# The vector engine's part of a depthwise convolution: one running sum in PSUM in place of two in SBUF

## The chip, the cores and the metric

The kernel runs on one core of a Trainium2 chip. The metric is the device time of one execution in microseconds (us), and lower is better. The engines of the core are TensorE (PE in the profile), VectorE (DVE), ScalarE (ACT), GpSimd (POOL) and SyncE (SP), which issues transfers. SBUF is the on-chip memory that all of them use; PSUM is the small memory, here used as eight banks of 128 partitions by 512 fp32 values, into which TensorE writes its products.

## The reference

Two streams of 256 tokens each, the latent tokens and a context, with 1024 channels in fp32, pass two layers: half a gated FFN, a token mixer, half a gated FFN. The mixer of layer 0 is a convolution module, that of layer 1 an attention; a final norm ends the latent stream. The change lies in the convolution module:

```
def conformer_conv(h, pw1_w, pw1_b, dw_w, dw_b, ln_g, ln_b, pw2_w, pw2_b):
    a = h @ pw1_w + pw1_b
    u, g = jnp.split(a, 2, axis=-1)
    u = u * jax.nn.sigmoid(g)
    u = lax.conv_general_dilated(
        u, dw_w[:, None, :].astype(u.dtype), window_strides=(1,),
        padding=[(CONV_PAD, CONV_PAD)], dimension_numbers=("NWC", "WIO", "NWC"),
        feature_group_count=D_MODEL) + dw_b
    uf = u.astype(jnp.float32)
    mu = jnp.mean(uf, axis=-1, keepdims=True)
    var = jnp.mean(jnp.square(uf - mu), axis=-1, keepdims=True)
    u = ((uf - mu) * lax.rsqrt(var + NORM_EPS)).astype(u.dtype) * ln_g + ln_b
    return jax.nn.silu(u) @ pw2_w + pw2_b
```

Each of the 1024 channels is convolved over time with 31 weights of its own (`dw_w`). Context and latent tokens are convolved separately.

## The kernel before

**Layout.** Channels lie on the 128 partitions, in eight chunks (c = 0 to 7); the free axis holds 512 tokens, latent first. Every matrix product in fp32 is three products of high and low halves (`mm3`: hi·hi, hi·lo, lo·hi). Weights come in by DMA, ACT writes the high half (`hi`), GpSimd subtracts it from the raw value (`lo`).

**The convolution module.** `pw1_mm` makes the products of the first pointwise layer for one chunk: a tile `u` and a tile `g`, each one PSUM bank (`ug` in the trace). `pw1_end` is the GLU: ACT takes the sigmoid of `g` (`sg`), VectorE multiplies it with `u` into the padded tile `U` in SBUF. After that U's chunk is convolved. The eight chunks are divided among the engines:

- VectorE takes chunks 0, 2 and 3 whole and the latent half of chunk 4 (its first 256 columns); it runs one SCALAR_TENSOR_TENSOR for each tap: the shifted U times the tap's weight, plus a running sum (`taps_v`).
- ACT and GpSimd take chunk 1 (`taps_p`): ACT multiplies, GpSimd adds.
- TensorE takes chunks 5, 6 and 7 and the context half of chunk 4 (`taps_t`), after `split_u` has split U into high and low halves.

In `taps_v` the running sum of a chunk is kept twice, in `A_`, which is the chunk's place in the result tile `Dt`, and in `B`, a work tile; both lie in SBUF. Even taps go to A_, odd ones to B. ACT makes the first tap of each (L706, L708). For chunks 3 and 4 the tap 1 also subtracts the mean shift K0 (L719). Chunk 0's first 20 taps (KS) go over each stream's 256 columns by themselves; everything else is 512 wide, and chunk 4's half 256. At the end L727 adds A_ and B; for chunk 2 L732 subtracts K0. Then `stats` adds the chunk to a running sum (L686), ACT squares it (L688), and VectorE adds the squares some taps later (L689).

**K0.** When chunk 0 is ended, `shift` (K) sums it over its partitions on TensorE (L935, output `pn`), and ACT writes K0 from that (L936, shown as `SK<-pn`). `first_stats` (D) subtracts K0 from chunk 0. The other chunks get K0 subtracted in `centre` (L819, L822) or as told above. `ln_stat` (s, L829) is the matmul on the finished sums, with which the LayerNorm of the latent stream begins.

**What sets the order.** Inside the convolution no scheduler works: a string of tokens, `SEQ2`, is run from left to right, and each engine gets its instructions in that order. `A`, `C` and `P` are the pointwise products of the latent half of chunks 0 and 1, the context half of these, and both halves of a later chunk; `l`, `m` and `E` are their GLUs; `v1` is one tap of VectorE from the queue `qv`, which holds the chunks 0, 2, 3 and 4 in turn; `R1` is a pair of taps of chunk 1; `T` are taps on TensorE; `L` and `h` load a weight block; `S` splits U; `K`, `D`, `F`, `s` as above. So a stretch around the end of chunk 0 reads `v1 v1 v1 h v1 L K v1 R1 v1 ...`, and an instruction that waits holds up all that comes after it on its engine. Outside the convolution a scheduler orders the work by dependencies and by the tiles that pools have free.

**Banks.** The pool `ps` has six PSUM banks in turn for all products (`ug`, and `o` of TensorE's taps), `pn` two for norms and statistics.

Of the kernel before, what the change touches and what calls it, by code (L numbers as in the profile page):

```python
# [11 lines left out]
F32 = mybir.dt.float32  # L12
# [3 lines left out]
ALU = mybir.AluOpType  # L16
# [69 lines left out]
def trunk(ctx, tc, a, out):  # L86
# [8 lines left out]
    small = ctx.enter_context(tc.tile_pool(name="small", bufs=2))  # L95
    ps = ctx.enter_context(tc.tile_pool(name="ps", bufs=6, space=bass.MemoryType.PSUM))
    pn = ctx.enter_context(tc.tile_pool(name="pn", bufs=2, space=bass.MemoryType.PSUM))
# [27 lines left out]
    def pcol(off, i):  # L125
        return par[:, off + i:off + i + 1]

# [1 line left out]
    stream = []  # L129
# [90 lines left out]

# [1 line left out]
    todo = [(0, t) for t in range(16, 72)] + [(1, t) for t in range(72)]  # L222
# [19 lines left out]

# [1 line left out]
    accj = const.tile([P, 2 * T], F32, name="accj")  # L244
# [98 lines left out]

# [1 line left out]
    XG = []  # L345
# [115 lines left out]

# [1 line left out]
    R0 = work.tile([P, 2, T], F32, tag="mt", name="R0")  # L463
# [3 lines left out]
    b1 = const.tile([P, CT], F32, name="b1")  # L467
    gu = [[ps.tile([P, 512], F32, tag="ps", name="gu") for _ in range(2)] for _ in range(NFF0)]
    chunks = []
# [64 lines left out]
    with tc.manual_schedule(engines=MS):  # L534
# [31 lines left out]
        def root(s):  # L566
            r = rs[s]
            nc.vector.tensor_reduce(out=r, in_=pc[:, 4 * s:4 * s + 4].rearrange("p (b h) -> p b h", h=2),
                                    axis=mybir.AxisListType.X, op=ALU.add)
            nc.gpsimd.tensor_tensor(out=r, in0=r, in1=nhalf[:, 0:2], op=ALU.pow)  # L570
# [55 lines left out]

# [1 line left out]
    ffn(0, 0, (0, 1), pre_ctx=None, mid=lambda: norm(0, 0, 1), per_block=lambda: ada(2 + (done[0] % 5 == 0)), begun=gu)  # L628

# [1 line left out]
    Dt = mp.tile([P, CT, 2 * T], F32, tag="mh", name="Dt")  # L631
# [9 lines left out]
    def pw1_mm(cs, kts, sl, first=True):  # L641
        """Products of the blocks cs over kts, all outputs of a kt before the next."""
        for kt in kts:
            for blk, u, g in cs:
                hi, lo = blk
                for q, dst in enumerate((u, g)):
                    o = (q * 8 + kt) * P
                    mm3(dst[:, :sl.stop - sl.start], hi[:, o:o + P], lo[:, o:o + P], HH[:, kt, sl], HL[:, kt, sl], kt == 0, kt == 7)
# [22 lines left out]
    def wk(c, k):  # L671
        return pcol(O_DWW, c * CW + k)

    def dview(c, a_, b_):
        return Dt[:, c, a_ * T:b_ * T].rearrange("p (s t) -> p s t", t=T)
# [15 lines left out]
    def step(n=1):  # L691
        for z in lag:
            z[0] -= n
        while lag and lag[0][0] <= 0:
            lag.pop(0)[1]()

    def taps_v(c, a_, b_, ks=0):
        A_ = dview(c, a_, b_)
        Bt = work.tile([P, 512], F32, tag="mt", name="B")
        B_ = Bt[:, a_ * T:b_ * T].rearrange("p (s t) -> p s t", t=T)  # L700

        def src(k, z=slice(a_, b_)):
            return UV[:, c, z, k:k + T]

        def first(z, d, e):
            nc.scalar.activation(out=d, in_=src(0, z), func=AF.Identity, scale=wk(c, 0), bias=pcol(O_DWB, c))  # L706
            if c in (0, 2):
                nc.scalar.activation(out=e, in_=src(1, z), func=AF.Copy, scale=wk(c, 1))  # L708
        if ks:
            for s in range(2):  # L710
                first(slice(s, s + 1), A_[:, s:s + 1], B_[:, s:s + 1])
                for k in range(2, ks):
                    d = (A_ if k % 2 == 0 else B_)[:, s]
                    nc.vector.scalar_tensor_tensor(out=d, in0=src(k, s), scalar=wk(c, k), in1=d, op0=ALU.mult, op1=ALU.add)
                    yield
        else:
            first(slice(a_, b_), A_, B_)
        if c not in (0, 2):
            nc.vector.scalar_tensor_tensor(out=B_, in0=src(1), scalar=wk(c, 1),  # L719
                                           in1=K0[:, a_ * T:b_ * T].rearrange("p (s t) -> p s t", t=T),  # L720
                                           op0=ALU.mult, op1=ALU.subtract)
            yield
        for k in range(max(2, ks), CW):
            d = A_ if k % 2 == 0 else B_
            nc.vector.scalar_tensor_tensor(out=d, in0=src(k), scalar=wk(c, k), in1=d, op0=ALU.mult, op1=ALU.add)  # L725
            yield
        nc.vector.tensor_tensor(out=A_, in0=A_, in1=B_, op=ALU.add)  # L727
        if c == 0:
            return
        yield  # L730
        if c == 2:
            nc.vector.tensor_tensor(out=Dt[:, c, :], in0=Dt[:, c, :], in1=K0, op=ALU.subtract)  # L732
            yield
        stats(c, a_, b_)
# [90 lines left out]
    def ln_stat(s):  # L825
        pc = pn.tile([P, 512], F32, tag="pn", name="pn")
        for z, o in ((S1[:, SL[s]], 0), (acc[s], 2)):
            for b in range(2):
                nc.tensor.matmul(pc[:, o + b:o + b + 1], z[:, b * P:(b + 1) * P], k1024, start=True, stop=True)  # L829
        return pc  # L830
# [64 lines left out]
    with tc.manual_schedule(engines=MS):  # L895
# [3 lines left out]
        def put(k, *v):  # L899
            st[k] = v[0] if len(v) == 1 else v  # L900
# [31 lines left out]

        def shift():
            pk = pn.tile([P, 512], F32, tag="pn", name="pn")
            nc.tensor.matmul(pk, ones, Dt[:, 0, :], start=True, stop=True)  # L935
            nc.scalar.activation(out=K0, in_=pk, func=AF.Copy, scale=1.0 / P)  # L936
# [5 lines left out]
        def tap(c, n):  # L942
            gen = st.setdefault(("t", c), taps_t(c))
            for _ in range(n):
                next(gen, None)

        def root():
# [11 lines left out]
            "F": lambda v: centre(v // 100, v // 10 % 10, v % 10), "Q": lambda c: stats(c, 0, 2), "z": step,  # L959
            "s": lambda _: put("pc", ln_stat(0)), "q": lambda _: root(), "M": lambda _: bcast(st["m"], st["R"][:, T:]),  # L960
            "W": lambda _: bcast(st["r"], st["R"]), "n": lambda c: put(("n", c), ln_scale(0, c, st["R"])),
            "o": lambda c: ln_low(0, c, st.pop(("n", c)))}
        for t in SEQ2.split():
            ops[t[0]](int(t[1:] or 0))
        st = None
    UHL.clear()
# [10 lines left out]

# [1 line left out]
    ffn(0, 2, (0, 1), pre_ctx=lambda: norm(1, 0, 2), mid=lambda: norm(0, 1, 0), per_block=lambda: ada(1))  # L979
    ffn(1, 0, (0, 1), pre_ctx=lambda: norm(1, 1, 0), mid=lambda: norm(0, 1, 1), per_block=lambda: ada(2))  # L980

# [1 line left out]
    cst = rawp.tile([P, 2048], F32, tag="raw", name="cst")  # L983
# [136 lines left out]

# [1 line left out]
    sq = ffn(1, 2, (0,), pre_ctx=None, mid=None, per_block=lambda: ada(1))  # L1122
# [112 lines left out]
```

## Time and profile before

| what | value |
|---|---|
| time of the runs | 1762.5, 1767.8, 1770.88 us; median 1767.8 us |
| span of the profiled execution, first to last instruction | 1767.2 us; it has no other time of its own, and is 0.6 us below the median |
| TensorE matmuls busy over the span | 1677.1 us (95%) |
| VectorE busy | 1193.3 us (68%) |
| GpSimd busy | 824.0 us (47%) |
| ACT busy | 632.4 us (36%) |
| mean granted clock of TensorE | 0.970 of full speed |

The span is one profiled execution, whose parts can be read; the runs' times are what a change is measured by. Shares over the whole span are means over stages with different limits. A row of the timeline gives a start and a duration, and in brackets how long the engine had been idle before, and the instruction that ended the wait.

### The profile page before, as it was taken

To read this page: it belongs to the slowest core of one execution; us is meant where nothing else is said; L and a number is where in the kernel's file an instruction comes from. 1 tells how busy PE (TensorE), PEld (TensorE's weight loads), DVE (VectorE), ACT (ScalarE), POOL (GpSimd) and SP (SyncE) were. 2 spreads that over 40 slices of the span, in tenths; PEclk is the share of its full clock that TensorE was granted. 3 is DMA by queue.
4 is the path that set the end of the run, shared out by engine and by line. 5 is a ranking of instruction groups with operands and counts; after the bars stand their busy time and mean duration, and the time that the engine had idled before them with its cause. 6 is when DMAs were issued, how large, how long until landed. Compare 5 with 4: busy or idle time off the path is not lost.

```text
span 1767.2 us, 23475 instructions
## 1 busy us (share of the span) xinstructions
PE 1677.1 (95%) x9229; PEld 1436.1 (81%) x9229; DVE 1193.3 (68%) x1792; ACT 632.4 (36%) x1074; POOL 824.0 (47%) x577
## 2 busy tenths in 40 slices
PE   8999999999676798999999999999999999989998
PEld 7788888879566698888888898888888897789997
DVE  3588889877999887554555565755553389756562
ACT  2522222234423574322222233212222346745443
POOL 1234223364867565656566555565565454230003
PEclk7999999999888899999999999999999999989999
DMA  7645466442112232434333332454553221236451
GB/s 268 227 168 217 180 218 238 175 149 73 48 48 95 96 132 96 153 133 142 132 137 134 134 119 97 190 185 166 182 190 111 90 72 49 74 128 229 171 194 66
DMA packets 48494, 252.13 MB, mean 143 GB/s; under 512 B 5248, under 2 KB 7296, under 8 KB 30848
## 3 DMA queue, kind: packets, MB, share of 16 engines
q1 hardware_dynamic: 48384, 250.64, 39.6%
q8 instruction: 72, 1.18, 0.3%
q14 instruction: 38, 0.31, 0.1%
HBM read 249.57 MB, written 1.05 MB: 142 GB/s over the span
## 4 chain that ended last, share of the span: by engine, by line
PE 70%; DVE 18%; issue 5%; ACT 3%; DMA 2%; POOL 2%; SPq 0%; POOLq 0%; DVEq 0%; ACTq 0%
PE o L213 8%; PE o L214 8%; PE o L215 8%; PE g L214 7%; PE g L215 7%; PE u L214 7%; PE g L213 7%; PE u L215 7%; PE u L213 7%; DVE Dt L725 3%; DVE B L725 3%; DVE junk L235 2%; PE gu L530 2%; POOL lo L177 1%; ACT hi L174 1%
## 5 line engine op out<-in xcount | busy, mean ns | idle before, releaser
L177 POOL TENSOR_TENSOR lo<-raw,hi 128x512 fp32r<-128x512 f32 (+1 forms) x416 | 639.3, 1567 | 706.5 <-ACT hi L174 566.2
L174 ACT ACTIVATE hi<-raw 128x1024 fp32r<-128x1024 f32 (+3 forms) x364 | 296.8, 872 | 577.7 <-PE u L214 254.8
L235 DVE CUSTOM_DVE_ANT_0 junk<-adaw,srow,par 128x1024 bf16<-128x1024 f32 x224 | 382.0, 1705 | 6.6 <-DMA adaw<-in_adaT 2.0
L213 PE MATMUL o<-MH,hi 128*128 128x512 f32 (+1 forms) x788 | 269.7, 344 | 4.3 <-ACT MH L218 4.3
L214 PE MATMUL o<-ML,hi 128*128 128x512 f32 (+1 forms) x788 | 269.8, 344 | 0.0
L215 PE MATMUL o<-MH,lo 128*128 128x512 f32 (+1 forms) x788 | 269.7, 344 | 0.0
L214 PE MATMUL g<-HL,hi 128*128 128x512 f32 (+1 forms) x712 | 254.8, 358 | 4.0 <-DVE HL L324 4.0
L213 PE MATMUL g<-HH,hi 128*128 128x512 f32 (+1 forms) x712 | 253.8, 358 | 3.1 <-ACT HH L320 3.1
L215 PE MATMUL g<-HH,lo 128*128 128x512 f32 (+1 forms) x712 | 254.4, 357 | 0.0
L215 PE MATMUL u<-HH,lo 128*128 128x512 f32 (+1 forms) x712 | 254.3, 357 | 0.0
L214 PE MATMUL u<-HL,hi 128*128 128x512 f32 (+1 forms) x712 | 254.3, 357 | 0.0
L213 PE MATMUL u<-HH,hi 128*128 128x512 f32 (+1 forms) x712 | 253.8, 357 | 0.0
L219 DVE TENSOR_TENSOR ML<-mt,MH 128x512 fp32r<-128x512 f32 (+1 forms) x92 | 104.7, 1138 | 120.8 <-ACT MH L218 120.5
L393 DVE TENSOR_TENSOR mt<-sg,u 128x512 f32<-128x512 f32 (+1 forms) x89 | 53.0, 596 | 179.6 <-PE u L215 163.1
L213 PEld LDWEIGHTS o<-MH,hi 128*128 128x128 f32 x788 | 149.2, 190 | 22.7 <-ACT MH L218 5.2
L341 DVE SCALAR_TENSOR_TENSOR X<-o,g,X 128x256 f32<-128x256 f32 x168 | 75.4, 479 | 131.7 <-PE o L215 131.5
L215 PEld LDWEIGHTS o<-MH,lo 128*128 128x128 f32 x788 | 149.8, 190 | 17.6
L214 PEld LDWEIGHTS o<-ML,hi 128*128 128x128 f32 x788 | 149.7, 190 | 17.7
L214 PEld LDWEIGHTS g<-HL,hi 128*128 128x128 f32 x712 | 134.0, 189 | 26.9 <-DVE HL L324 5.3
L213 PEld LDWEIGHTS g<-HH,hi 128*128 128x128 f32 x712 | 134.2, 189 | 25.8 <-ACT HH L320 4.3
L213 PEld LDWEIGHTS u<-HH,hi 128*128 128x128 f32 x712 | 134.4, 189 | 21.6
L215 PEld LDWEIGHTS g<-HH,lo 128*128 128x128 f32 x712 | 134.4, 189 | 21.6
(208 smaller groups left out, 2676.1 us busy)
## 6 DMA issues: line engine op xcount, KB each, us to landing
raw<-in_wi SPq DMA_DIRECT2D x85, 1024.0 KB, 4.8
adaw<-in_adaT SPq DMA_DIRECT2D x128, 512.0 KB, 3.7
raw<-in_wo SPq DMA_DIRECT2D x32, 896.0 KB, 4.7
raw<-in_wo SPq DMA_DIRECT2D x20, 1024.0 KB, 5.2
raw<-in_pw SPq DMA_DIRECT2D x12, 1024.0 KB, 4.8
raw<-in_dwd SPq DMA_DIRECT2D x8, 1024.0 KB, 4.8
ch<-in_ada SPq DMA_DIRECT2D x6, 1024.0 KB, 12.7
raw<-in_qkv SPq DMA_DIRECT2D x6, 1024.0 KB, 4.8
```

The source lines that it names most:

```text
L174: nc.scalar.activation(out=hi[:, q:q + w], in_=raw[:, q:q + w], func=AF.Copy)
L177: eng.tensor_tensor(out=lo[:, z:e], in0=raw[:, z:e], in1=hf[:, z:e], op=ALU.subtract)
L213: nc.tensor.matmul(o, wh, xh, start=first, stop=False)
L214: nc.tensor.matmul(o, wh, xl, start=False, stop=False)
L215: return nc.tensor.matmul(o, wl, xh, start=False, stop=last)
L219: return i_, nc.vector.tensor_tensor(out=lo, in0=src, in1=hif, op=ALU.subtract)
L235: nc.vector.tensor_tensor_reduce(out=junk, in0=wt, in1=srow[:, s, :], scale=1.0, scalar=pcol(O_ADAB, 72 * l + t), op0=ALU.mult, op1=ALU.ad ...
L341: return nc.vector.scalar_tensor_tensor(out=X[:, c, SL[s]], in0=psrc, scalar=gate, in1=X[:, c, SL[s]], op0=ALU.mult, op1=ALU.add)
L393: nc.vector.tensor_tensor(out=mt[:, :n], in0=sg[:, :n], in1=u[:, :n], op=ALU.mult)
L530: nc.tensor.matmul(gu[k][q], w[:, o:o + P], h[:, c, :], start=c == 0 and h is HH and w is hi, stop=c == 7 and w is lo)
L725: nc.vector.scalar_tensor_tensor(out=d, in0=src(k), scalar=wk(c, k), in1=d, op0=ALU.mult, op1=ALU.add)
```

## The change

The pool `ps` gets five banks, and a new pool `pv` one: it holds a tile `A`, in which VectorE keeps a single running sum. Every tap of `taps_v` reads A and writes A in place; tap 0 is a TENSOR_SCALAR on VectorE (U times its weight), so ACT's first taps are gone, and so are B and the addition at the end. When the taps of a chunk have ended, one instruction writes Dt from A: for chunk 0 it adds the bias, for the others it adds the bias and subtracts K0 in one SCALAR_TENSOR_TENSOR. As the next chunk uses the same bank, its tap 0 waits for that instruction. The number of yields in a chunk's taps has changed, so a `v1` late in the string stands for another tap than before: `K` now runs VectorE's taps until chunk 0 has ended, and `s` first runs what is left. At the start of the kernel one tile of the first FFN's products (`gu`) lies in the new pool. The rest of the diff is comments that are left out.

```
-    ps = ctx.enter_context(tc.tile_pool(name="ps", bufs=6, space=bass.MemoryType.PSUM))
+    ps = ctx.enter_context(tc.tile_pool(name="ps", bufs=5, space=bass.MemoryType.PSUM))
+    pv = ctx.enter_context(tc.tile_pool(name="pv", bufs=1, space=bass.MemoryType.PSUM))
...
-    gu = [[ps.tile([P, 512], F32, tag="ps", name="gu") for _ in range(2)] for _ in range(NFF0)]
+    gu = [[pv.tile([P, 512], F32, tag="pv", name="gu") if 2 * k + q == 5 else ps.tile([P, 512], F32, tag="ps", name="gu")
+           for q in range(2)] for k in range(NFF0)]
...
+    ended = set()
+
     def taps_v(c, a_, b_, ks=0):
-        A_ = dview(c, a_, b_)
-        Bt = work.tile([P, 512], F32, tag="mt", name="B")
-        B_ = Bt[:, a_ * T:b_ * T].rearrange("p (s t) -> p s t", t=T)
+        At = pv.tile([P, 512], F32, tag="pv", name="A").rearrange("p (s t) -> p s t", t=T)
 
         def src(k, z=slice(a_, b_)):
             return UV[:, c, z, k:k + T]
 
-        def first(z, d, e):
-            nc.scalar.activation(out=d, in_=src(0, z), func=AF.Identity, scale=wk(c, 0), bias=pcol(O_DWB, c))
-            if c in (0, 2):
-                nc.scalar.activation(out=e, in_=src(1, z), func=AF.Copy, scale=wk(c, 1))
+        def taps(k0, k1, z=slice(a_, b_)):
+            for k in range(k0, k1):
+                d = At[:, z]
+                if k == 0:
+                    nc.vector.tensor_scalar(out=d, in0=src(k, z), scalar1=wk(c, k), scalar2=None, op0=ALU.mult)
+                else:
+                    nc.vector.scalar_tensor_tensor(out=d, in0=src(k, z), scalar=wk(c, k), in1=d, op0=ALU.mult, op1=ALU.add)
+                yield
+
         if ks:
             for s in range(2):
-                first(slice(s, s + 1), A_[:, s:s + 1], B_[:, s:s + 1])
-                for k in range(2, ks):
-                    d = (A_ if k % 2 == 0 else B_)[:, s]
-                    nc.vector.scalar_tensor_tensor(out=d, in0=src(k, s), scalar=wk(c, k), in1=d, op0=ALU.mult, op1=ALU.add)
-                    yield
...
-        nc.vector.tensor_tensor(out=A_, in0=A_, in1=B_, op=ALU.add)
+                yield from taps(0, ks, slice(s, s + 1))
+        yield from taps(ks, CW)
+        d, e = dview(c, a_, b_), At[:, a_:b_]
+        ended.add(c)
         if c == 0:
+            nc.vector.tensor_scalar(out=d, in0=e, scalar1=pcol(O_DWB, c), scalar2=None, op0=ALU.add)
             return
+        nc.vector.scalar_tensor_tensor(out=d, in0=e, scalar=pcol(O_DWB, c), in1=K0[:, a_ * T:b_ * T].rearrange("p (s t) -> p s t", t=T),
+                                       op0=ALU.add, op1=ALU.subtract)
         yield
-        if c == 2:
-            nc.vector.tensor_tensor(out=Dt[:, c, :], in0=Dt[:, c, :], in1=K0, op=ALU.subtract)
-            yield
         stats(c, a_, b_)
...
         def shift():
+            while 0 not in ended:
+                qv.pump(1)
...
+        def closed():
+            qv.pump(99)
+            step(9)
...
-            "s": lambda _: put("pc", ln_stat(0)), "q": lambda _: root(), "M": lambda _: bcast(st["m"], st["R"][:, T:]),
+            "s": lambda _: (closed(), put("pc", ln_stat(0))), "q": lambda _: root(), "M": lambda _: bcast(st["m"], st["R"][:, T:]),
```

The order of VectorE's instructions where the taps begin, in the kernel before. `U<-ug,par,sg` is the GLU's product, and what stands in brackets is the engine that the instruction waits for:

```order
L668 SCALAR_TENSOR_TENSOR U<-ug,par,sg 128x256 [waits Activation_49] x2
L714 SCALAR_TENSOR_TENSOR Dt<-U,par,Dt 128x256 [waits Activation_49]
L714 SCALAR_TENSOR_TENSOR B<-U,par,B 128x256 [waits Activation_49]
L714 SCALAR_TENSOR_TENSOR Dt<-U,par,Dt 128x256 [waits DVE_49]
L714 SCALAR_TENSOR_TENSOR B<-U,par,B 128x256 [waits DVE_49]
L668 SCALAR_TENSOR_TENSOR U<-ug,par,sg 128x256 [waits Activation_49]
```

The same place and what follows it, to the end of chunk 0, after the change. The rows of a group now read and write one tile, A:

```order
L711 TENSOR_SCALAR A<-U,par 128x256 [waits DVE_49]
L713 SCALAR_TENSOR_TENSOR A<-U,par,A 128x256 [waits DVE_49] x3
L670 SCALAR_TENSOR_TENSOR U<-ug,par,sg 128x256 [waits Activation_49]
L713 SCALAR_TENSOR_TENSOR A<-U,par,A 128x256 [waits DVE_49] x5
L670 SCALAR_TENSOR_TENSOR U<-ug,par,sg 128x256 [waits Activation_49]
L713 SCALAR_TENSOR_TENSOR A<-U,par,A 128x256 [waits DVE_49] x11
L711 TENSOR_SCALAR A<-U,par 128x256 [waits DVE_49]
L713 SCALAR_TENSOR_TENSOR A<-U,par,A 128x256 [waits DVE_49] x16
L670 SCALAR_TENSOR_TENSOR U<-ug,par,sg 128x256 [waits Activation_49]
L670 SCALAR_TENSOR_TENSOR U<-ug,par,sg 128x256
L713 SCALAR_TENSOR_TENSOR A<-U,par,A 128x256 [waits DVE_49] x3
L713 SCALAR_TENSOR_TENSOR A<-U,par,A 128x512 [waits DVE_49] x11
```

The waits for ACT's first taps are gone. Before, a tap waited for the one two places ahead of it; now each waits for the one directly ahead, and the next two instructions are the writing of Dt from A (L723) and chunk 2's tap 0. After the change VectorE runs 71 taps of 256 columns and 73 of 512 there, with four such endings; before, it ran 65 of 256 and 69 of 512 at L714 and L725, two at L719, and five additions and subtractions of the whole chunk.

On TensorE, the context products of chunk 1 begin in the kernel before at the row that waits; `ug` are the tiles in banks of `ps`, and the second such wait belongs to the second tile:

```order
L213 MATMUL ug<-HH,hi 128x256 [waits Activation_49]
L214 MATMUL ug<-HL,hi 128x256
L215 MATMUL ug<-HH,lo 128x256
L213 MATMUL ug<-HH,hi 128x256 [waits Activation_49]
L214 MATMUL ug<-HL,hi 128x256
```

And after the change:

```order
L214 MATMUL ug<-HH,hi 128x256 [waits Activation_49]
L215 MATMUL ug<-HL,hi 128x256
L216 MATMUL ug<-HH,lo 128x256
L214 MATMUL ug<-HH,hi 128x256 [waits DVE_49]
L215 MATMUL ug<-HL,hi 128x256
```

No matmul has moved there. The second tile waited for ACT and now waits for VectorE, as it takes a bank that a GLU product of the latent half has to read first.

## Rows read from the trace of the kernel before

**Rows 1.** The page: TensorE's busy time; shares of the chain that ended last.
```profile
PE 1677.1 (95%) x9229; PEld 1436.1 (81%) x9229; DVE 1193.3 (68%) x1792; ACT 632.4 (36%) x1074; POOL 824.0 (47%) x577
PE 70%; DVE 18%; issue 5%; ACT 3%; DMA 2%; POOL 2%; SPq 0%; POOLq 0%; DVEq 0%; ACTq 0%
```

**Rows 2.** Windows: us, busy us of PE, PEld, DVE, ACT, POOL; PE clock; DMA.
```profile
437.50:609.10 171.60, 120.23 (x647) 103.34 (x646) 167.50 (x184) 66.21 (x112) 120.52 (x85) 0.84 0.21 74
470.00:480.00 10.00, 0.00 (x0) 0.00 (x0) 9.97 (x19) 4.55 (x6) 4.71 (x1) 0.50 0.00 1
...
650.00:1100.00 450.00, 442.19 (x2278) 374.20 (x2277) 254.32 (x349) 144.73 (x224) 253.28 (x169) 1.00 0.35 124
1450.00:1500.00 50.00, 49.41 (x314) 40.65 (x312) 46.64 (x129) 34.08 (x83) 22.98 (x25) 1.00 0.13 46
```

**Rows 3.** Timeline, TensorE: start us, duration us, instruction [idle before, what ended it].
```profile
431.98 0.58 PE L214 MATMUL ug<-HL,hi 128*128 128x256 f32 x1 [2.34 <-DVE HL L324]
...
481.51 2.04 PE L935 MATMUL pn<-Dt,onesr 128*128 128x512 f32 x2 [15.10 <-DVE Dt L727]
...
518.04 0.77 PE L213 MATMUL ug<-HH,hi 128*128 128x512 f32 x1 [10.14 <-DVE U L668]
...
609.08 1.01 PE L829 MATMUL pn<-k,SK 128*128 128x1 f32 x4 [7.83 <-DVE SK L686]
```

**Rows 4.** Groups by form, VectorE, 430 to 635 us: busy us, mean ns | idle.
```profile
L725 DVE SCALAR_TENSOR_TENSOR Dt<-U,par,Dt 128x512 f32<-128x512 f32 x36 | 44.1, 1225 | 0.0
L725 DVE SCALAR_TENSOR_TENSOR B<-U,par,B 128x512 f32<-128x512 f32 x33 | 39.0, 1183 | 0.1
L714 DVE SCALAR_TENSOR_TENSOR B<-U,par,B 128x256 f32<-128x256 f32 x18 | 18.1, 1006 | 0.0
L714 DVE SCALAR_TENSOR_TENSOR Dt<-U,par,Dt 128x256 f32<-128x256 f32 x18 | 17.9, 994 | 1.6 <-ACT Dt L706 1.6
L725 DVE SCALAR_TENSOR_TENSOR Dt<-U,par,Dt 128x256 f32<-128x256 f32 x15 | 14.3, 957 | 0.1
L725 DVE SCALAR_TENSOR_TENSOR B<-U,par,B 128x256 f32<-128x256 f32 x14 | 13.8, 988 | 0.0
```

**Rows 5.** Timeline, VectorE: two pairs of neighbouring taps.
```profile
469.96 0.47 DVE L714 SCALAR_TENSOR_TENSOR Dt<-U,par,Dt 128x256 f32<-128x256 f32 x1
470.36 0.47 DVE L714 SCALAR_TENSOR_TENSOR B<-U,par,B 128x256 f32<-128x256 f32 x1
...
500.21 0.75 DVE L725 SCALAR_TENSOR_TENSOR Dt<-U,par,Dt 128x512 f32<-128x512 f32 x1
500.88 1.79 DVE L725 SCALAR_TENSOR_TENSOR B<-U,par,B 128x512 f32<-128x512 f32 x1
```

**Rows 6.** Timeline, GpSimd, at the same time as the last pair.
```profile
500.80 3.03 POOL L155 TENSOR_TENSOR lo<-raw,hi 128x512 fp32r<-128x512 f32 x2 [8.15 <-ACT hi L152]
```

**Rows 7.** One line (L317), whole kernel: duration ns, least/median/most; pn lies in PSUM.
```profile
L317 DVE SCALAR_TENSOR_TENSOR t<-X,A,pn x72: 464/473/484, 414.4 to 1572.7; 128x256 f32<-128x256 f32 x72
```

**Rows 8.** Timeline, VectorE: two pairs, the second of each reading the first's result.
```profile
517.82 0.68 DVE L727 TENSOR_TENSOR Dt<-Dt,B 128x512 f32<-128x512 f32 x1
518.53 0.69 DVE L732 TENSOR_TENSOR Dt<-Dt,SK 128x512 f32<-128x512 f32 x1
...
615.45 0.42 DVE L844 TENSOR_TENSOR t<-Dt,pn 128x256 f32<-128x256 f32 x1 [1.51 <-PE pn L262]
615.91 0.42 DVE L845 TENSOR_TENSOR t<-t,pn 128x256 f32<-128x256 f32 x1
```

**Rows 9.** Timeline, VectorE: GLU products of chunks 0 and 1, 2, 5 and 7.
```profile
435.00 0.88 DVE L668 SCALAR_TENSOR_TENSOR U<-ug,par,sg 128x256 f32<-128x256 f32 x2 [0.71 <-ACT sg L653]
...
472.21 0.86 DVE L668 SCALAR_TENSOR_TENSOR U<-ug,par,sg 128x256 f32<-128x256 f32 x2
...
523.38 1.98 DVE L661 SCALAR_TENSOR_TENSOR U<-ug,par,sg 64x256 f32<-64x256 f32 x4 [1.99 <-ACT sg L653]
...
580.90 1.98 DVE L661 SCALAR_TENSOR_TENSOR U<-ug,par,sg 64x256 f32<-64x256 f32 x4
```

**Rows 10.** Waits of GpSimd, 430 to 635 us: total us, times, longest us.
```profile
POOL lo L155 <- ACT hi L152: 46.4, 11, 8.8
```

More of the change, by code (lines that the diff above doesn't have):

```diff
@@ L709, in taps_v @@
         if ks:
             for s in range(2):
-                first(slice(s, s + 1), A_[:, s:s + 1], B_[:, s:s + 1])
-                for k in range(2, ks):
-                    d = (A_ if k % 2 == 0 else B_)[:, s]
-                    nc.vector.scalar_tensor_tensor(out=d, in0=src(k, s), scalar=wk(c, k), in1=d, op0=ALU.mult, op1=ALU.add)
-                    yield
[L716 to L721, printed above, removed]
-            yield
@@ L723, in taps_v @@
[L723 to L726, printed above, removed]
-        nc.vector.tensor_tensor(out=A_, in0=A_, in1=B_, op=ALU.add)
+                yield from taps(0, ks, slice(s, s + 1))
+        yield from taps(ks, CW)
+        d, e = dview(c, a_, b_), At[:, a_:b_]
+        ended.add(c)
         if c == 0:
+            nc.vector.tensor_scalar(out=d, in0=e, scalar1=pcol(O_DWB, c), scalar2=None, op0=ALU.add)
@@ L729, in taps_v @@
             return
+        nc.vector.scalar_tensor_tensor(out=d, in0=e, scalar=pcol(O_DWB, c), in1=K0[:, a_ * T:b_ * T].rearrange("p (s t) -> p s t", t=T),
+                                       op0=ALU.add, op1=ALU.subtract)
         yield
-        if c == 2:
-            nc.vector.tensor_tensor(out=Dt[:, c, :], in0=Dt[:, c, :], in1=K0, op=ALU.subtract)
-            yield
         stats(c, a_, b_)
@@ L964, in trunk @@
             ops[t[0]](int(t[1:] or 0))
+        assert not qv.gens and not qp.gens and not lag
         st = None
```

## The prediction

> **What bounds the kernel now.** Read first the shares of the chain of work that ended last. TensorE holds 70% of it and VectorE 18% [rows 1]; a VectorE share that large in a kernel of matrix products means that somewhere TensorE waits for VectorE. The table of windows says where. From 650 to 1100 us TensorE is busy 442.19 of 450 us, so there it is the bound. From 437.50 us (the first VectorE tap) to 609.10 us it is busy only 120.23 of 171.60 us, at a granted clock of 0.84, while VectorE is busy 167.50 us; from 470 to 480 us TensorE does nothing and its clock stands at 0.50, the lower of its two levels [rows 2]. In the convolution VectorE is the bound. TensorE's own timeline names the waits: 15.10 us for the sum that ends chunk 0's taps, 10.14 us for VectorE's GLU product of chunk 3, which gives a PSUM bank back, and 7.83 us for the last statistics before the LayerNorm at 609.08 us [rows 3]. So the question is how soon VectorE gets to that last point, and then whether what follows can use the lead.
>
> **What a tap costs now.** By form, the 69 taps of 512 elements take 1225 and 1183 ns on average and the 65 of 256 elements 957 to 1006 ns; together 44.1 + 39.0 + 18.1 + 17.9 + 14.3 + 13.8 = 147.2 us [rows 4], and two more at L719. The mean hides two kinds. Alone, a tap of 256 takes 0.47 us and the next starts 0.40 us after it; a tap of 512 takes 0.75 and the next starts 0.67 us later. But the tap that starts at 500.88 us takes 1.79 us [rows 5], and 500.80 us is when GpSimd starts two subtractions that take 3.03 us [rows 6]. The slow taps lie under GpSimd's work and the quick ones beside its pauses. Both of a tap's tensors, the shifted U and the running sum, lie in SBUF. The row that tells what a PSUM operand does is that of the norm's L317: the same operation and form, one tensor input in SBUF and one in PSUM, 72 times all over the kernel, 464 to 484 ns [rows 7]. It is never stretched, and it costs no more than the 0.47 us of a quiet tap. So a tap whose running sum comes from PSUM should not be stretched under GpSimd. Here only its input side is shown; a VectorE instruction that writes its result into PSUM is in no row.
>
> **The change, part by part.**
> *The chain.* Two alternating sums let a tap start before its predecessor has ended: steps of 0.40 and 0.67 for durations of 0.47 and 0.75. With one sum each tap waits for the one before. What such a dependent step costs is in two pairs: L844 takes 0.42 and L845, which reads its result, starts 0.46 after it; L727 takes 0.68 and L732 starts 0.71 after it [rows 8]. That is the duration and 0.03 to 0.04 more, so a chained tap takes 0.47 + 0.04 = 0.51 and 0.75 + 0.03 = 0.78 us. The loss against an uncontended tap is 0.11 us, for 144 taps 16 us, and it is inside these two prices.
> *The sum.* After, 71 taps of 256 elements and 73 of 512 run on VectorE: 71 x 0.51 + 73 x 0.78 = 93.1, and four ends at about 0.7, together 96. Before, the 147.2 us, 1.2 for L719 and some 4 for the additions overlap by about 0.075 us for each of 136 taps (10 us), so they hold 142 us. VectorE gets 46 us back in the convolution, ACT loses eight first taps, which it did beside other work, and I count those at nothing.
> *What a store into PSUM costs* no row shows. From below: nothing, as L317's PSUM input costs nothing. From above: two rows of one tap form give a fixed part of 2 x 0.47 - 0.75 = 0.19 us; were the fixed part paid half again, 0.10 us for each tap, 144 x 0.10 = 14 us. I take 0.03, nearer to L317's row, which is of the same form: 4 us.
>
> *Where the 46 us go.* I walk VectorE's new order from one meeting with another engine to the next.
> - Start. The context product of chunk 1 gets its banks later with five in the pool: its second tile waits for a VectorE GLU product of the latent half, where before it began some five matmuls (1 us) after 431.98 [rows 3]. Those products run from 435.00 to 435.88 [rows 9], so the context products come about 3 us late, and the taps between them cannot start earlier. The last of them is at about 448, and 28 chained taps of 256 follow: 14 us. Chunk 2's GLU is at 463 against 472.21 [rows 9], a lead of 9.
> - Chunk 0's end. 0.9 + 3 x 0.51 + 11 x 0.78 + 0.7 = 11.7 us later, at 475, against 481.51 [rows 3]: a lead of 6.5, because the stretch before it had few stretched taps in it. TensorE's 15.10 us of waiting shrink to some 8.
> - Chunk 2's taps, 25 x 0.78, and two statistics end at 496. TensorE is through P4 and P5 (48 matmuls of 512 columns each, 10.9 us at the full clock) by 499, so P6 starts there in place of 518.04 [rows 3], and chunk 5's GLU at 501 to 502 in place of 523.38 [rows 9]: a lead of 21, VectorE waiting some 2 us for P5.
> - Up to chunk 7's GLU VectorE has 33 taps of 512 (25.7), 5 of 256 (2.6), and 12.5 us of GLU products, splits and statistics that stay: 41, so it is there at 543 against 580.90 [rows 9], a lead of 37.
> - From there to the statistics the old kernel takes 28 us, half of it TensorE's taps of chunk 7, their spread on ACT and the last centring. VectorE's remaining taps shorten by some 9 us, but that chain does not; I keep the 28 us. The statistics' matmul is at 572 in place of 609.08: 37 us earlier.
>
> *Does the rest follow?* TensorE has 576 matmuls of the products P2 to P7 and of chunks 5 to 7 and some 70 of chunk 4 to do by then. At 0.227 and 0.12 us that is 288 x 0.227 + 359 x 0.12 = 108 us of the 134 left, so it is close behind but not the bound. GpSimd has 120.52 us of work there [rows 2], part of which is itself stretched, and 46.4 us in which its subtraction waits for ACT's high half [rows 10], which waits for a buffer that TensorE frees. After the LayerNorm TensorE is 98% busy and does the same work, so a lead there is kept to the end.
>
> *One bank less elsewhere.* In attention five live tiles are often wanted, but TensorE is busy 49.41 of 50 us there [rows 2]; by counting live tiles, few instructions must wait for a sixth. Bounds: nothing, and some 10 us if each of the attention's groups waited a microsecond. I take 2.
>
> *Sum:* 37 - 4 - 2 = 31 us off the profiled execution. Its span is 1767.2 us, 0.6 below the median of the runs shown, so 1736.2 and 0.6: **1737 us**.
>
> **Rivals.**
> A. *Another engine's order takes over.* Chunks 5 to 7 pass through TensorE, ACT, VectorE and TensorE again, with five banks instead of six, and GpSimd's additions of chunk 1 stay where they are in its queue. For it: the 108 of 134 us above leave little room for waits, and each earlier station trims a wait that was only masked. Against it: TensorE's largest waits all name VectorE. If a third to two thirds of the lead goes, the gain is 10 to 24 us: 1744 to 1757, say 1750.
> B. *A tap through PSUM has a dearer fixed part.* The mechanism: each of the 144 taps reads and writes PSUM, and the chain pays its latency every time. At half the fixed part again the sum is 37 - 14 - 2 = 21, and if the dependent step grows by as much as the duration does, some 18 to 20 more is lost at the stations: about 1753. The row of L317, 473 ns with a PSUM input, speaks against the reading half of it; nothing speaks on the writing half. [...]
> C. *Slower: the round trip.* In a chain of one sum the next tap can start only when the last element of its predecessor is in the bank and can be read back. Break-even is where the added time for each of 144 taps eats the lead: 35 / 144 = 0.24 us, a step of 0.75 and 1.02 us. If the store and the return each cost the fixed part of 0.19 again, the step grows by 0.38, VectorE loses 55 us and is some 20 us later than now: about 1788. For it: nothing in this kernel chains through PSUM. Against it: the dependent pairs cost only 0.03 to 0.04 over the duration [rows 8].
> D. *It does not do what it says*, since a tap with its sum in PSUM is stretched under GpSimd all the same. Then the chain is only a loss, 16 us of it on a stage where VectorE is the bound: about 1784. L317's maximum of 484 ns in 72 places [rows 7] makes it unlikely.
>
> **How the numbers follow.** The forecast (a gain of 24 to 42 us) gets 0.53, A 0.22, B 0.11 (it overlaps A's times), a gain above 42 us 0.05, hardly any change because several of A's waits add up 0.04, C 0.03, D 0.02. Faster by over 0.5%, which is about what a measurement of this kernel can tell from no change, means below 1759: the first four, less 0.03 of A and B that land above it, 0.88. Within 0.5%: 0.07. Slower: 0.05. The range has to reach over the forecast, A and B: 1725 to 1757.
>
> **What would show it.** In the profile after, the tap rows should read about 0.47 and 0.75 us with minimum and maximum close together, none above 1 us, and steps of 0.51 and 0.78. If their duration stands near 0.57 and 0.85, it is B; if steps are far above the durations, C; if maxima near 1.8 remain, D. TensorE's wait ahead of the mean-shift product should fall from 15 to about 8 us, its wait for the last statistics should move to about 572 us, and its clock over the stage should rise from 0.84. If that matmul comes after 585 us with quick taps, rival A is at work, and the longest wait before it names the engine. The windows from 650 us on should keep TensorE's busy share; a lower share in attention would mean that the sixth bank was worth more than I count. GpSimd's subtractions should shorten as well, as the contention goes both ways.

## The result, and the profile after

The changed kernel takes 1738.43 us (median; 1736.98 to 1741.44) against 1767.53 us for the kernel before in the same runs. The ratio is 0.9842, with a 95% interval of 0.9826 to 0.9857: 29 us faster, where 31 were forecast, 1737 us. The profiled execution has a span of 1735.3 us.

The page of the kernel after, its busy times and the shares of the chain that ended last, answers to [rows 1]:

```profile
PE 1675.5 (97%) x9229; PEld 1433.8 (83%) x9229; DVE 1142.3 (66%) x1799; ACT 628.7 (36%) x1066; POOL 800.6 (46%) x577
...
PE 79%; DVE 10%; issue 4%; ACT 3%; POOL 2%; DMA 2%; POOLq 0%; DVEq 0%; SPq 0%; ACTq 0%
```

VectorE's share of the chain has gone from 18% to 10%. It has not gone to nothing: the convolution is still a stage in which VectorE is waited for. VectorE's groups by form, 425 to 600 us of the kernel after (columns as in [rows 4]):

```profile
L713 DVE SCALAR_TENSOR_TENSOR A<-U,par,A 128x512 f32<-128x512 f32 x71 | 53.6, 755 | 2.3
L713 DVE SCALAR_TENSOR_TENSOR A<-U,par,A 128x256 f32<-128x256 f32 x68 | 33.2, 488 | 2.0
...
L711 DVE TENSOR_SCALAR A<-U,par 128x512 f32<-128x512 f32 x2 | 1.5, 748 | 0.0
L711 DVE TENSOR_SCALAR A<-U,par 128x256 f32<-128x256 f32 x3 | 1.5, 484 | 0.1
```

The means have fallen from about 1200 to 755 ns and from about 990 to 488 ns, and the view of line L713 alone gives 477 as the least and 757 as the most of both forms (durations: least/median/most), so no tap is stretched:

```profile
L713 DVE SCALAR_TENSOR_TENSOR A<-U,par,A x139: 477/747/757, 433.3 to 567.1; 128x512 f32<-128x512 f32 x71, 128x256 f32<-128x256 f32 x68
```

The steps follow from the timeline, in which equal neighbours are joined. Sixteen taps of 256 take 8.27 us from 452.21 to the GLU at 460.48, 0.517 us each; fourteen of 512 take 10.95 us from 482.03 to 492.98, 0.782 us each. The forecast had 0.51 and 0.78.

```profile
452.21 8.36 DVE L713 SCALAR_TENSOR_TENSOR A<-U,par,A 128x256 f32<-128x256 f32 x16
460.48 0.87 DVE L670 SCALAR_TENSOR_TENSOR U<-ug,par,sg 128x256 f32<-128x256 f32 x2
...
482.03 11.04 DVE L713 SCALAR_TENSOR_TENSOR A<-U,par,A 128x512 f32<-128x512 f32 x14
492.98 0.87 DVE L670 SCALAR_TENSOR_TENSOR U<-ug,par,sg 128x256 f32<-128x256 f32 x2
...
498.90 1.98 DVE L663 SCALAR_TENSOR_TENSOR U<-ug,par,sg 64x256 f32<-64x256 f32 x4 [2.01 <-ACT sg L655]
...
540.57 1.98 DVE L663 SCALAR_TENSOR_TENSOR U<-ug,par,sg 64x256 f32<-64x256 f32 x4
```

TensorE's longest waits in that stage (engine, line, what it waited for: us in total, times, longest), and the windows of the convolution, of the piece ahead of K and of the attention's projections. Behind them stands the one window of the kernel before that answers to the last:

```profile
PE pn L823 <- DVE SK L688: 8.0, 1, 8.0
PE ug L214 <- ACT sg L655: 6.6, 1, 6.6
PE pn L931 <- DVE Dt L723: 5.0, 1, 5.0
```

```profile
432.75:568.65 135.90, 121.10 (x681) 105.20 (x680) 119.04 (x191) 63.89 (x108) 99.31 (x87) 0.94 0.29 101
466.00:476.00 10.00, 5.03 (x13) 2.99 (x13) 9.57 (x13) 2.54 (x4) 9.76 (x9) 0.72 0.24 77
1377.90:1406.00 28.10, 23.47 (x160) 20.14 (x159) 23.61 (x52) 13.03 (x24) 17.19 (x13) 0.99 0.21 76
```

```profile
1417.20:1439.30 22.10, 21.01 (x158) 19.84 (x157) 18.95 (x44) 10.22 (x20) 12.25 (x9) 1.00 0.27 96
```

From the first tap to the last statistics the stage now takes 135.90 us in place of 171.60 [rows 2], 35.7 less. TensorE stands still for 14.8 us of it in place of 51.4, and its granted clock there is 0.94 in place of 0.84. But there is a loss far behind it: the same 150 matmuls of the attention's projections take 28.10 us where they took 22.10.

The best way to see both is the lead: the start of TensorE's n-th matmul, counted from its first, in the kernel before minus that in another kernel. All have 9229 matmuls. The table is worked out from the starts in the traces, in us, and the versions are those of the next section:

| n, and what it stands for | changed | e1 | e2 | e7 | e8 | e9 | e10 |
|---|---|---|---|---|---|---|---|
| 1950, ahead of the context products | 3.2 | -0.9 | -1.4 | -1.0 | 0.5 | 0.8 | 0.1 |
| 2100, P2 | -1.0 | -5.2 | -5.7 | -5.4 | 0.3 | 0.6 | -0.1 |
| 2700, end of the convolution's taps | 40.5 | -5.4 | 35.7 | 44.6 | 50.3 | 42.2 | 50.0 |
| 6750, attention's projections begin | 39.3 | -6.0 | 34.3 | 42.4 | 49.7 | 46.1 | 53.1 |
| 6900, 150 matmuls later | 33.3 | -12.3 | 34.3 | 42.4 | 49.7 | 46.1 | 53.2 |
| 7500, attention | 30.6 | -14.9 | 35.2 | 42.7 | 50.2 | 46.7 | 54.2 |
| 9228, the last | 31.7 | -14.4 | 36.0 | 43.9 | 50.7 | 47.2 | 54.9 |

The changed kernel has 3.2 us at matmul 1950, nearly all of it from the first 31 us; e3, whose first products are the same, has 0.4 there, so this is how that execution happened to start and no gain of the change. From there on: 4.2 us lost at the context products, 41.5 gained in the convolution, 8.7 lost from the attention's projections up to the middle of the attention (1.2 more before these, and 1.1 back behind them).

### The profile page after: what moved, and what is told of

It reads as the page before. It is cut to its first block, busy times and chain, and to the rows that moved or that the text cites. A ratio compares the mean times of both kernels' runs of the same rounds, so it can differ in the third digit from the quotient of the medians.

```text
span 1735.3 us, 23481 instructions
## 1 busy us (share of the span) xinstructions
PE 1675.5 (97%) x9229; PEld 1433.8 (83%) x9229; DVE 1142.3 (66%) x1799; ACT 628.7 (36%) x1066; POOL 800.6 (46%) x577
## 4 chain that ended last, share of the span: by engine, by line
PE 79%; DVE 10%; issue 4%; ACT 3%; POOL 2%; DMA 2%; POOLq 0%; DVEq 0%; SPq 0%; ACTq 0%
PE o L215 8%; PE o L214 8%; PE o L216 8%; PE g L215 8%; PE u L215 8%; PE g L216 8%; PE g L214 8%; PE u L214 7%; PE u L216 7%; DVE A L713 3%; PE gu L532 2%; DVE HL L325 1%; POOL lo L178 1%; PE ug L214 1%; ACT hi L175 1%
## 5 line engine op out<-in xcount | busy, mean ns | idle before, releaser
L216 PEld LDWEIGHTS o<-MH,lo 128*128 128x128 f32 x788 | 150.0, 190 | 17.8
L215 PEld LDWEIGHTS o<-ML,hi 128*128 128x128 f32 x788 | 149.9, 190 | 17.9
L215 PEld LDWEIGHTS u<-HL,hi 128*128 128x128 f32 x712 | 134.1, 188 | 21.7
```

The lines of the kernel that those rows point to most:

```text
L215: nc.tensor.matmul(o, wh, xl, start=False, stop=False)
L216: return nc.tensor.matmul(o, wl, xh, start=False, stop=last)
```

## The experiments

**e3: the place of the sum alone.**

```
-        At = pv.tile([P, 512], F32, tag="pv", name="A").rearrange("p (s t) -> p s t", t=T)
+        At = work.tile([P, 512], F32, tag="mt", name="A").rearrange("p (s t) -> p s t", t=T)
```

> The changed kernel with one edit: the single running sum lies in an SBUF tile, everything else as in the changed kernel (five banks, no first taps on ACT, the one-instruction ending). Theory (the gain is the place of the sum, as a tap with both tensors in SBUF is stretched under GpSimd): taps of 512 between 0.75 and 1.8 us and of 256 between 0.47 and 1.5 us, as before, and each link dearer by 0.11 us, for 144 taps 16 us: slower than before, 1775 to 1795 us. Rival (the gain comes from the single sum: no additions at the end, no first taps on ACT): about 1738 us.

Measured: 1786.24 us, ratio to before 1.0109 (1.0092 to 1.0126). Its taps by form, and the view of its line L713 (durations: least/median/most):

```profile
L713 DVE SCALAR_TENSOR_TENSOR A<-U,par,A 128x512 f32<-128x512 f32 x71 | 81.1, 1142 | 2.3
L713 DVE SCALAR_TENSOR_TENSOR A<-U,par,A 128x256 f32<-128x256 f32 x68 | 61.6, 906 | 2.1
```

```profile
L713 DVE SCALAR_TENSOR_TENSOR A<-U,par,A x139: 476/833/1832, 437.0 to 617.8; 128x512 f32<-128x512 f32 x71, 128x256 f32<-128x256 f32 x68
```

One line of the source is 48 us. The single sum, the missing first taps and the one-instruction ending are all in e3, and it is slower than before, by 19 us. The time falls into the expected range, but not for the reason given there: 15.6 of the 19 us are the price of the lost bank, which e3 shares with e1 below, and against e1 the chained sum in SBUF costs 3.8 us and not 16. The least duration is the same, 476 against 477 ns; what differs is the most, 1832 against 757 ns.

**e4 and e5: GpSimd's additions taken away, without and with the change.** The edit is the same in both:

```
-                for q in range(2):
-                    nc.gpsimd.tensor_tensor(out=A_, in0=A_, in1=pr[:, q, :n], op=ALU.add)
```

> The kernel before, without GpSimd's additions of chunk 1 (L747), so chunk 1 keeps its first tap alone; ACT's products for it stay. This takes away 36.2 + 16.5 = 52.7 us of the 120.5 us that GpSimd works beside the taps. Theory (GpSimd's work stretches each VectorE tap beside it): the taps of before lie 147.2 - 65 x 0.47 - 69 x 0.745 = 65 us above their quiet durations; if 44% of that goes, VectorE has 28 us less and the time falls by 20 to 28 us, to 1740 to 1747 us. Rival (the taps are slow for a reason of their own, as two sums in turn): within 5 us of before.

Measured: 1738.85 us, ratio 0.9852 (0.9828 to 0.9876), 27 us below before.

> The changed kernel, without the same additions of GpSimd. Theory (a tap with its sum in PSUM is not touched by GpSimd): tap durations as they are, 0.49 and 0.755 us, and the time within 4 us of the changed kernel, 1734 to 1738 us. Rival (GpSimd still holds the stage up, by its own queue): 10 us or more below it.

Measured: 1740.02 us, ratio 0.9849 (0.9832 to 0.9866); the changed kernel has 0.9842. Chunk 0's taps of 256 in e4, which took 18.1 and 17.9 us in the kernel before, its taps of 512, which took 44.1 and 39.0 [rows 4], and the 512-wide taps of e5:

```profile
L714 DVE SCALAR_TENSOR_TENSOR B<-U,par,B 128x256 f32<-128x256 f32 x18 | 9.6, 534 | 0.0
L714 DVE SCALAR_TENSOR_TENSOR Dt<-U,par,Dt 128x256 f32<-128x256 f32 x18 | 9.0, 501 | 1.6 <-ACT Dt L706 1.6
...
L725 DVE SCALAR_TENSOR_TENSOR Dt<-U,par,Dt 128x512 f32<-128x512 f32 x36 | 39.1, 1085 | 0.0
L725 DVE SCALAR_TENSOR_TENSOR B<-U,par,B 128x512 f32<-128x512 f32 x33 | 36.1, 1094 | 0.1
```

```profile
L713 DVE SCALAR_TENSOR_TENSOR A<-U,par,A 128x512 f32<-128x512 f32 x71 | 53.6, 755 | 2.3
```

With both sums in SBUF, taking work from GpSimd takes 27 us off the kernel; with the sum in PSUM it takes nothing off, and the taps' 53.6 us are the same to the tenth. The taps of 512 are only in part relieved in e4, as GpSimd's subtractions (L155, 88.3 us from 430 to 620 us) stay there. So it is GpSimd's work that stretched the taps, and the change is what shields them.

A count over the traces says the same. Call a tap stretched when it takes over 0.52 us (256 elements) or 0.80 us (512), and covered when GpSimd works for more than half of it. In the kernel before, all 76 stretched taps are covered, and of the 60 others 10 are. In the changed kernel 113 of 139 taps are covered, and none is stretched.

The relief is mutual, as forecast: GpSimd's subtraction (L155 of before, L156 after) fell from 1512 to 1326 ns and its 512-wide addition from 1810 to 1310.

**e1 and e2: the bank.** e1 is the kernel before with five banks for products and the sixth unused by the taps; e2 is the changed kernel with six, the sum being taken from that pool while the taps run. The diff is e2's against the changed kernel; e1 has its first three lines the other way round, in the kernel before, and nothing else but the start's `gu` tile in `pv`.

```
-    ps = ctx.enter_context(tc.tile_pool(name="ps", bufs=5, space=bass.MemoryType.PSUM))
-    pv = ctx.enter_context(tc.tile_pool(name="pv", bufs=1, space=bass.MemoryType.PSUM))
+    ps = ctx.enter_context(tc.tile_pool(name="ps", bufs=6, space=bass.MemoryType.PSUM))
...
-        At = pv.tile([P, 512], F32, tag="pv", name="A").rearrange("p (s t) -> p s t", t=T)
+        At = ps.tile([P, 512], F32, tag="ps", name="A").rearrange("p (s t) -> p s t", t=T)
```

> The kernel before with one edit: five banks in the pool for products, the sixth in a pool that the taps do not use (both running sums stay in SBUF). Theory (the lost bank is paid in the attention): the lead of TensorE's matmuls over the kernel before is unchanged up to the attention and falls there by the 8 us that the changed kernel loses there (39 us of lead before it, 31 behind it), so about 1775 us. Rival 1 (those 8 us came from how the scheduler happened to draw the attention of the changed kernel, not from the bank): about 1767 us. Rival 2 (the convolution needs the sixth bank as well, and the changed kernel only hides that): 1780 us or more, with waits for banks between 430 and 610 us.

Measured: 1782.49 us, ratio 1.0094 (1.0076 to 1.0112), 15.6 us slower than before. That is the second rival: the table shows 4.3 us of it at the context products and 8.9 us in the attention. The first of these two losses is a wait of TensorE that the changed kernel has too, of 6.6 us for `sg`.

> The changed kernel, with the running sum taken from the pool of products, which has its six banks again: only while the taps run does one of them hold the sum. Theory (the bank is missed in the attention alone): the convolution as in the changed kernel, the attention as before, about 1738 - 8 = 1730 us. Rival (the scheduler's draw): about 1738 us, with the 8 us still lost in the attention.

Measured: 1730.79 us, ratio 0.9800 (0.9785 to 0.9814), as the theory had it. Between matmuls 6750 and 7500, where the changed kernel loses 8.7 us, e2 loses nothing (34.3 and 35.2). It still loses 4.3 at the context products, because its sum takes a bank there as well.

**e7: the price of the chain.** Two alternating sums again, but both in PSUM, on top of e2; an instruction more per chunk adds them.

```
+        At, Bt = (p.tile([P, 512], F32, tag=t, name=n).rearrange("p (s t) -> p s t", t=T)
+                  for p, t, n in ((ps, "ps", "A"), (pn, "pn", "B")))
...
+                d = (At, Bt)[k % 2][:, z]
...
+        nc.vector.tensor_tensor(out=d, in0=d, in1=f, op=ALU.add)
```

> As the version with six banks, but with two alternating sums, both in PSUM (the second in the pool of the norms), added at the end by one more VectorE instruction for each chunk. It prices the chain of one sum. Theory (a tap waits for the whole of the one before, 0.11 us for each of 144 taps, and VectorE still sets the pace of the convolution): steps of 0.40 and 0.67 us, VectorE 16 - 3 = 13 us shorter, and the time 8 to 13 us below that of the version with six banks, about 1718 to 1722 us. Rival 1 (TensorE's and ACT's own order is the bound by now): within 3 us of that version, about 1730 us. Rival 2 (two neighbours in PSUM do not overlap): steps of 0.50 and 0.78 and a time some 3 us above it.

Measured: 1723.13 us, ratio 0.9755 (0.9740 to 0.9769), 7.7 us below e2. Neighbouring taps of its timeline:

```profile
484.66 0.74 DVE L712 SCALAR_TENSOR_TENSOR A<-U,par,A 128x512 f32<-128x512 f32 x1
485.32 0.74 DVE L712 SCALAR_TENSOR_TENSOR B<-U,par,B 128x512 f32<-128x512 f32 x1
```

Durations stay at 0.74, steps are 0.66, against 0.782 with one sum: the chain's 0.12 us for each tap is what two sums save in PSUM; for SBUF [rows 5] and [rows 8] gave 0.11. For 144 taps that is about 17 us, less some 2.5 for the four additions; of these roughly 15 us, an estimate from the steps, the kernel got 7.7.

**e6: is VectorE still the pace?** In the changed kernel, the last 15 taps of chunk 3 are left out:

```
-        yield from taps(ks, CW)
+        yield from taps(ks, CW if c != 3 else 16)
```

> The changed kernel, with the last 15 taps of chunk 3 left out: 15 x 0.78 = 11.7 us less of VectorE between the GLU products of chunks 5 and 7. Theory (VectorE still sets the pace of the convolution): 8 to 12 us below the changed kernel, 1726 to 1730 us. Rival (TensorE's and ACT's order is the bound by now): within 3 us of it. In between, as with two sums in PSUM, where 13 us of VectorE gave 8: both hold in turn, 6 to 8 us.

Measured: 1730.48 us, ratio 0.9798 (0.9780 to 0.9816), 8 us below the changed kernel for 11.7 us of VectorE. It lies at the edge between the theory and the case in between. With e7 (7.7 of about 15) the reading is that half to two thirds of what VectorE saves now reaches the end, and the rest is lost on the way; where all of it goes is not shown. In e7 a part of it is seen: VectorE's wait for chunk 5's sigmoid is 3.4 us there, against 2.0 in the changed kernel.

**e8: who gets which bank.** On top of e7, in the order string:

```
-R1 v1 v1 v1 C1 C0
+R1 C1 v1 v1 v1 C0
```

> The version with two sums in PSUM, with one edit: the order string names the context product of chunk 1 (C1) ahead of the first three taps, so that its two tiles get the two free banks before the running sum does. No engine's own order changes, only who gets which bank. In all versions with the sum in PSUM TensorE waits 6.6 us there for ACT's sigmoid of the latent half, which reads the bank that the second tile takes. Theory (that wait delays the context products, the taps behind them and all that follows): TensorE waits there for the context's norm as in the kernel before, 4 us less, and the time falls by 3 to 5 us, to about 1719 us. Rival (the taps have other waits to fill that gap with): within 1 us of 1723.

Measured: 1718.39 us, ratio 0.9729 (0.9713 to 0.9745), 4.7 us below e7. TensorE's wait of 6.6 us for `sg` became the one of before [rows 3]:

```profile
431.51 0.39 PE L214 MATMUL ug<-HL,hi 128*128 128x256 f32 x1 [2.35 <-DVE HL L324]
```

**e9 and e10: taps moved into waits.** On top of e8:

```
-C0 L v1 m1
+C0 L v1 v5 m1
...
-H70 F701
+H70 v3 F701
```

> The version with the context product first, with VectorE's taps moved into its waits by two edits of the order string: five taps ahead of the GLU product of chunk 1's context half, for whose sigmoid VectorE waits 2.4 us, and chunk 4's end ahead of the last centring. So the five taps, the ending, the sum and the squares (about 4 us) that stood between the last centring and the statistics' matmul are done before. Theory (what VectorE does right ahead of that matmul is paid in full, since TensorE waits 7 us there): 3 to 4 us less, about 1715 us. Rival (the last centring waits for ACT's spread of chunk 7, and everything before it only fills that wait): within 1.5 us of 1718.

Measured: 1721.10 us, ratio 0.9747 (0.9728 to 0.9767): 2.7 us slower than e8, against both expectations. TensorE's waits show why: the running sums of chunk 3 were begun before P5 was named, and P5's second tile got a bank that chunk 3's GLU had to leave first.

```profile
PE ug L213 <- DVE U L668: 5.4, 1, 5.4
PE pn L824 <- DVE SK L686: 3.7, 1, 3.7
```

The wait ahead of the statistics had shrunk as meant, from 7.2 to 3.7 us. So e10 mends the bank alone:

```
-E3 R1 v1 v1 v1 P4 L P5 v1 R1 E5
+E3 R1 P4 L P5 v1 v1 v1 v1 R1 E5
```

> The version with the taps in the waits, with one edit: the order string names the products of chunks 4 and 5 (P4, P5) directly behind chunk 3's GLU (E3), ahead of the taps that begin the next running sums. In the version before it those sums were begun earlier and took the bank that P5's second tile had had; TensorE waited 5.4 us there for chunk 3's GLU and lost 8 us of lead at that point, which hid what the moved taps gave at the end (lead from 42 to 46 us over the last stretch, against 50 to 51). Theory (the loss was that bank alone): P5 waits as in the version with the context first, and the time is 2 to 5 us below that one's 1718.4, 1713 to 1716 us. Rival (the earlier taps bring nothing, as TensorE sets the pace there): 1717 to 1719 us.

Measured: 1712.95 us, ratio 0.9692 (0.9665 to 0.9720), the fastest version here: 54 us below the kernel before and 25 below the changed one.

## Why the prediction was right, and where it was not

**The tap.** Right in mechanism and size. The row that decided was L317 [rows 7], the same operation with an input in PSUM, which takes 484 ns at most in 72 places and so is never stretched; e3, e4 and e5 show that this is the reason and not the shorter program. The chained steps of 0.51 and 0.78 came as worked out from [rows 8], and the store, which no row of before showed, costs 488 - 473 = 15 ns against L317's median [rows 7] and 755 - 746 = 9 ns against the median of the old line L725, under 2 us in all where I had taken 4 and bounded by 14:

```profile
L725 DVE SCALAR_TENSOR_TENSOR Dt<-U,par,Dt x51: 471/746/1792, 471.5 to 602.1; 128x512 f32<-128x512 f32 x36, 128x256 f32<-128x256 f32 x15
```

Rival B, a dearer fixed part, did not happen: the whole difference in duration is 9 to 15 ns. (Its time does not follow from its own sum either: 21 us off is 1747, and with 18 to 20 more lost some 1766, not 1753.) Rivals C and D are excluded by the durations and steps above.

**The walk.** The changed kernel's execution runs 3.2 us early at the start of the stage; with that added, chunk 2's GLU stands at 463.6 (forecast 463), K at 475.5 (475), chunk 5's GLU at 502.1 (501 to 502), chunk 7's at 543.7 (543), the statistics at 571.8 (572). TensorE's wait for K fell to 5.0 us, not 8, as I had not let the delay of the context products reach TensorE itself: 15.1, less a lead of 6 at K, less 4.2 by which TensorE comes later, is 4.9. From 466 to 476 us its granted clock was 0.72, with 5.03 of 10 us busy, where in the kernel before it had stood still from 470 to 480 us, at 0.50 [rows 2]; the records of both traces hold two levels of it, 0.50 and 1.00.

**The context products: about the right price, the wrong wait.** Ahead of the prediction and in it I read the second wait of the order's piece on TensorE as one in chunk 1's context product. It is that of chunk 0, which follows it; chunk 1's begins 48 matmuls earlier, and there the new wait is for ACT's sigmoid of the latent half, 6.6 us in place of 2.3 us for the norm. The cost I took was 3 us, by a product of VectorE that was not the cause; 4.2 was measured, and e8 shows which wait it was.

**The sixth bank: mis-sized.** I took 2 us for the attention, from TensorE's busy share and a count of live tiles, with 10 as the upper bound. It costs 8.7 in the changed kernel and 8.9 in e1, and e2 gets it back. The step that failed is the reading of the busy share: a TensorE busy 49.41 of 50 us [rows 2] says that it has no waits now, not that it would have none with fewer banks. The loss lies mostly ahead of that window, in the projections, where I had looked at no row: 28.10 us for what took 22.10.

All 6 us of it are in the 48 matmuls of 512 columns with which the third weight block is multiplied, 24 for each of its two output tiles. Their window in the changed kernel with a stretch of it, the window in the kernel before, and rows of TensorE, the last of them from the kernel before:

```profile
1395.09:1413.04 17.95, 14.41 (x50) 9.75 (x49) 15.47 (x41) 7.09 (x14) 5.44 (x5) 0.90 0.34 117
1405.70:1409.10 3.40, 3.40 (x10) 2.63 (x9) 3.40 (x12) 0.75 (x2) 0.71 (x1) 0.50 0.47 128
1434.37:1446.19 11.82, 11.48 (x51) 8.86 (x49) 9.81 (x22) 4.74 (x8) 5.45 (x5) 1.00 0.25 89
```

```profile
1395.09 0.39 PE L214 MATMUL o<-HH,hi 128*128 128x512 f32 x1
...
1397.72 0.50 PE L215 MATMUL o<-HL,hi 128*128 128x512 f32 x1 [0.77 <-DVE HL L325]
...
1402.40 0.49 PE L214 MATMUL o<-HH,hi 128*128 128x512 f32 x1 [1.07 <-ACT HH L321]
1403.91 0.50 PE L215 MATMUL o<-HL,hi 128*128 128x512 f32 x1 [1.02 <-DVE HL L325]
```

```profile
1434.37 0.63 PE L213 MATMUL o<-HH,hi 128*128 128x512 f32 x2
```

With six banks the two output tiles are worked on in turn, as two products with `HH` in a row show, so each piece of the norm's result (`HH`, `HL`) feeds both when it comes. With five banks the order is `HH`, `HL`, `HH` throughout: one tile's 24 matmuls run first, each as its piece comes, and the other's behind them. TensorE then waits 3.5 us in all for the norm, against 0.34 before, and right behind these waits, from 1405.7 to 1409.1 us, its granted clock is 0.50, where it was 1.00 before; a matmul starts 0.43 us after the last there, in place of 0.23. The five kernels with five banks (the changed one, e1, e3, e5, e6) need 17.8 to 18.8 us for these 48 matmuls, the seven with six banks 11.3 to 11.8. Of the other 2.7 us, 2.1 are lost at the attention's first scores, with a wait of 1.35 us in place of 0.59 and the clock at 0.50 for 3.4 us more.

**The sum.** 37 - 4 - 2 = 31 was forecast. Measured against the lead at the start of the stage, it is 41.5 - 4.2 = 37 for the convolution, where the forecast had 37 - 4 = 33 (the walk's 37 had the delay in it, and the store cost under 2), and 8.7 in place of 2 lost behind: 28.6, and 29 by the medians. So the closeness of the total is partly luck, two errors of 4 and 7 us that offset each other.

**Rival A** did not happen, but it is near: e6 and e7 give half to two thirds of VectorE's further savings.

## What to carry to other kernels

Where a long VectorE chain of two-tensor operations runs beside GpSimd, look whether some rows are two to three times their least duration (here 1.79 us against 0.75 for a tap of 512), and whether the same operation with an operand in PSUM stays at the least (here 464 to 484 ns): then move the running tensor to PSUM and keep two of them in turn, as a chain of one costs the part that neighbours overlap (here 0.12 us for each tap). A bank for it should be borrowed for the stage and not for the kernel, and in an order written by hand the first mention decides who gets which bank: name the products that must not wait ahead of the tile that can. A stage with no waits tells little about how it will do with a bank less: here one bank less let two products that shared their inputs run one behind the other, 17.95 us in place of 11.82. The cheapest test is the old kernel with that bank taken away.

## What was not expected of the hardware

Tap 0, a TENSOR_SCALAR with one tensor input, is dearer into PSUM: 748 ns for 512 elements. In e3, from SBUF to SBUF, the same instruction took 477 ns (groups by form):

```profile
L711 DVE TENSOR_SCALAR A<-U,par 128x256 f32<-128x256 f32 x3 | 2.6, 867 | 0.0
...
L711 DVE TENSOR_SCALAR A<-U,par 128x512 f32<-128x512 f32 x2 | 1.0, 477 | 0.0
```

So this one-tensor operation, by two rows each, pays 0.27 us for a result in PSUM, while the two-tensor operation pays 9 to 15 ns. The first row shows the other side: three of 256 elements with a mean of 867 ns, from 346 to 1426 by the view of that line. In SBUF this form, too, is sometimes three or four times as long as at its least; that GpSimd is the cause was not tried for it.
